# The first MLP product of a decoder layer by one level of Strassen's algorithm, with its output and the residual kept in DRAM

## The chip, the cores and the metric

One core of a Trainium2 chip runs the whole program. The metric is device time in microseconds, the median of three runs. The profile of one more execution shows the core's engines: TensorE (PE, with its weight loads as PEld), VectorE (DVE), ScalarE (ACT), GpSimd (POOL) and SyncE (SP), which issues most DMAs.

## The reference

The reference is one layer of a hybrid decoder on 1024 prompt tokens and 64 sample tokens (8 sequences of 8), 1088 columns in all. Only the end of the layer matters here:

```
x = x + gt * (merged @ lp["w_out"])
sh, sc, gt = ada_mod(c, lp["w_ada_mlp"], lp["b_ada_mlp"])
h = rms_norm(x, lp["norm_mlp"]) * (1 + sc) + sh
x = x + gt * (jnp.square(jax.nn.relu(h @ lp["w_ff1"])) @ lp["w_ff2"])
y = rms_norm(x, W["norm_final"])
```

`x` has 1024 features, `w_ff1` is 1024 by 4096 and `w_ff2` 4096 by 1024, all in fp32.

## The kernel before

**Layout.** Features lie on the 128 partitions, tokens along the free axis: `x`, `h` and the merged branch are 8 tiles of 128 x 1088, the hidden activations 32. Every product is done in three passes: an fp32 operand is split into a high part (an ACT copy to fp32r) and a low part (a DVE or POOL subtraction), and `mm3` multiplies high by high, high by low and low by high into one PSUM bank. A product's 1088 columns go in three chunks of 364, 362 and 362 (`CH`). One output block of the first MLP product takes 8 input blocks x 3 chunks x 3 passes = 72 matmuls; 32 blocks make 2304. The second product also has 2304.

**Weights.** `weights` loads 128 x 512 through the SP queue and splits it. In the second phase four such split sets exist, so a set is loaded and split four jobs' halves ahead, into the buffers of the set that has just been used up.

**Order.** TensorE's instructions are in the order in which the Python program emits them; a small clock (`Pace`) that counts estimated matmul time decides while building where the steps of the generators (`norm2`, `ada`) fall between the matmuls. The order on the other engines and in the DMA queues is made by the framework's scheduler. Each engine and queue works strictly in its own order: an instruction that waits holds up those behind it.

**Second phase (`phase2`).** The merge (`or_job`) writes the split merged branch; `out_job(m, 0)` forms output block m of the out-projection for the first 726 columns, `out_job(m, 1)` for the last 362, and the result is added to the residual tiles `xr`, which stay in SBUF. `norm2(0)` and `norm2(1)` sum the squares of each part, and when the statistics have gone through TensorE (`stats`, `rms`), scale, modulate and split it. While `norm2(0)` works, TensorE does the 192 matmuls of `out_job(m, 1)`; while `norm2(1)` works, it does the first two chunks of three hidden blocks. After that the two MLP products alternate: four hidden blocks (`ff1_job`, whose `consume` applies ReLU, squares and splits each chunk straight from PSUM), then the second product of the four hidden blocks before (`ff2_jobs`), added to `xr`. The hidden blocks never leave SBUF. The last group of the second product runs in `last`, with the final norm behind it. `ada` forms the modulation vectors; its third part (`g == 2`, the MLP's gate) starts when `norm2(1)` is done.

**SBUF.** `hx` (16 tiles of 128 x 1088) holds the eight `xr` tiles and hidden blocks, `ma`/`mb` the split operands of 726 and 362 columns, `t` has 4 work tiles, `hid` 4. **PSUM.** Tags `mm` (4 banks), `w` (2) and `wc` (2) live for the whole program.

## Time and profile before

| | us |
|---|---|
| median of 3 runs (1751.83 to 1753.74) | 1752.13 |
| span of the profiled execution | 1744.2 |
| median less that span | 7.9 |
| merge (bound by loads of `d_th`), some 780 to 850 us | 70 |
| out-projection and norms, some 850 to 965 us | 115 |
| both MLP products, 965 us to the end | 779 |

The share of busy time in a row tells how long instructions of an engine were under way. A matmul's record lasts longer than the distance to the next one (matmuls overlap), so the pace of TensorE is read from the starts: from first to last start of a group, divided by the matmuls between. Idle time of an engine other than TensorE costs nothing as long as TensorE does not wait for it.

### The profile page before, as it was taken

To read this page: it belongs to the slowest core of one execution; us is meant where nothing else is said; L and a number is where in the kernel's file an instruction comes from. 1 tells how busy PE (TensorE), PEld (TensorE's weight loads), DVE (VectorE), ACT (ScalarE), POOL (GpSimd) and SP (SyncE) were. 2 spreads that over 40 slices of the span, in tenths; PEclk is the share of its full clock that TensorE was granted. 3 is DMA by queue.
4 is the path that set the end of the run, shared out by engine and by line. 5 is a ranking of instruction groups with operands and counts; after the bars stand their busy time and mean duration, and the time that the engine had idled before them with its cause. 6 is when DMAs were issued, how large, how long until landed. Compare 5 with 4: busy or idle time off the path is not lost.

```text
span 1744.2 us, 32136 instructions
## 1 busy us (share of the span) xinstructions
PE 1686.4 (97%) x13462; PEld 1573.4 (90%) x13462; DVE 845.4 (48%) x1550; ACT 550.8 (32%) x1108; POOL 282.3 (16%) x379
## 2 busy tenths in 40 slices
PE   6999999999999999999899999999999999999997
PEld 3989879887888798799798999999999999999997
DVE  5677375746574654344337633324333333333355
ACT  5442343434343434122225521213121212212133
POOL 3310111000000000016215411111201111111121
PEclk9999999998999999999999999999999999999999
DMA  9333314232313332858742411111111111111112
GB/s 338 106 108 131 113 66 136 87 108 85 126 52 124 99 120 96 301 174 306 251 152 86 133 49 43 43 49 43 43 49 43 43 48 44 43 44 48 43 43 104
DMA packets 80785, 179.58 MB, mean 103 GB/s; under 512 B 11360, under 2 KB 25696, under 8 KB 80640
## 3 DMA queue, kind: packets, MB, share of 16 engines
q1 hardware_dynamic: 72960, 155.63, 26.5%
q10 hardware_dynamic: 6048, 16.23, 2.8%
q0 software_dynamic: 1632, 5.67, 1.0%
q8 instruction: 106, 1.74, 0.4%
q14 instruction: 39, 0.32, 0.1%
HBM read 138.64 MB, written 38.84 MB: 102 GB/s over the span
## 4 chain that ended last, share of the span: by engine, by line
PE 87%; DVE 6%; DMA 3%; ACT 2%; issue 1%; POOL 1%; SPq 0%; ACTq 0%; DVEq 0%; POOLq 0%
PE mm L170 58%; PE w L170 23%; PE wc L170 4%; DMA t<-d_th 2%; PE w L177 1%; POOL t L1344 1%; DMA x<-in_xT 1%; DVE t L1403 0%; DMA hid<-in_w_ada_mlp 0%; DVE ma L1405 0%; DVE mb L1348 0%; DVE wt L680 0%; DVE wlo L190 0%; DVE h L461 0%; DVE acc L1383 0%
## 5 line engine op out<-in xcount | busy, mean ns | idle before, releaser
L170 PE MATMUL mm<-hx,whi 128*128 128x362 f32 (+2 forms) x2608 | 679.6, 342 | 4.3 <-ACT px L564 1.6
L170 PEld LDWEIGHTS mm<-hx,whi 128*128 128x128 f32 x2608 | 455.8, 190 | 40.9 <-issue 17.8
L170 PE MATMUL mm<-hx,wlo 128*128 128x362 f32 (+3 forms) x1304 | 428.9, 329 | 0.0
L189 ACT ACTIVATE whi<-wraw 128x512 fp32r<-128x512 f32 x246 | 155.1, 630 | 535.6 <-PE w L170 356.0
L170 PE MATMUL mm<-ma,whi 128*128 128x364 f32 (+1 forms) x1280 | 318.7, 330 | 3.1 <-ACT ma L1347 2.6
L170 PEld LDWEIGHTS mm<-hx,wlo 128*128 128x128 f32 x1304 | 248.4, 190 | 0.1
L170 PEld LDWEIGHTS mm<-ma,whi 128*128 128x128 f32 x1280 | 226.7, 188 | 12.1 <-issue 8.4
L190 POOL TENSOR_TENSOR wlo<-wraw,whi 128x512 fp32r<-128x512 f32 x91 | 120.0, 1319 | 669.7 <-ACT whi L189 669.7
L170 PE MATMUL mm<-ma,wlo 128*128 128x364 f32 (+1 forms) x640 | 210.4, 329 | 0.2 <-DVE wlo L190 0.2
L190 DVE TENSOR_TENSOR wlo<-wraw,whi 128x512 fp32r<-128x512 f32 x155 | 109.1, 704 | 207.9 <-ACT whi L189 207.6
L1552 DVE SCALAR_TENSOR_TENSOR hx<-mm,aq,hx 128x364 f32<-128x364 f32 (+3 forms) x136 | 75.0, 587 | 206.5 <-PE mm L170 206.4
L170 PE MATMUL w<-mb,whi 128*128 128x362 f32 x576 | 143.8, 331 | 0.0
L170 PEld LDWEIGHTS mm<-ma,wlo 128*128 128x128 f32 x640 | 120.6, 189 | 0.5 <-DVE wlo L190 0.5
L1427 DVE TENSOR_TENSOR ft<-ft 128x362 f32<-128x362 f32 (+1 forms) x96 | 53.1, 576 | 130.3 <-ACT ft L1426 129.8
L170 PEld LDWEIGHTS w<-mb,whi 128*128 128x128 f32 x576 | 102.6, 191 | 2.5 <-issue 1.7
L170 PE MATMUL w<-hx,whi 128*128 128x362 f32 x416 | 102.8, 328 | 0.1
L170 PE MATMUL w<-mb,wlo 128*128 128x362 f32 x288 | 95.5, 332 | 2.7 <-DVE wlo L190 2.7
L170 PE MATMUL mm<-hid,whi 128*128 128x364 f32 (+4 forms) x304 | 74.9, 328 | 0.0
L170 PEld LDWEIGHTS w<-hx,whi 128*128 128x128 f32 x416 | 73.2, 189 | 1.3 <-POOL hx L466 0.8
L1426 ACT ACTIVATE ft<-mm 128x364 f32<-128x364 f32 x64 | 29.5, 475 | 125.5 <-PE mm L170 125.4
L170 PE MATMUL w<-hx,wlo 128*128 128x362 f32 x208 | 67.4, 324 | 0.0
L1557 POOL TENSOR_TENSOR hx<-hx,rs 128x64 f32<-128x64 f32 x72 | 39.3, 546 | 143.2 <-DVE rs L1555 143.1
(330 smaller groups left out, 2173.1 us busy)
## 6 DMA issues: line engine op xcount, KB each, us to landing
wraw<-in_w_ff SPq DMA_DIRECT2D x134, 256.0 KB, 2.6
wraw<-in_w_in SPq DMA_DIRECT2D x68, 256.0 KB, 3.0
hid<-in_w_ada_mlp SPq DMA_DIRECT2D x24, 512.0 KB, 4.5
d_th<-px SPq DMA_DIRECT2D x22, 544.0 KB, 3.0
wt<-d_x SPq DMA_DIRECT2D x20, 544.0 KB, 4.3
t<-d_th ACTq DMA_DIRECT2D x16, 544.0 KB, 6.4
aw<-in_w_ada_mix SPq DMA_DIRECT2D x16, 512.0 KB, 9.2
wraw<-in_w_out SPq DMA_DIRECT2D x32, 256.0 KB, 2.9
```

Of the source, the lines that this page charges most:

```text
L170: return self.nc.tensor.matmul(out, lhsT, rhs, **kw)
L177: self.nc.tensor.transpose(out, in_, ident)
L189: nc.scalar.activation(hi, raw, AF.Copy)
L190: (nc.gpsimd if n < 2 or n % 2 and n >= self.solo else nc.vector).tensor_tensor(lo, raw, hi.bitcast(F32), op=ALU.subtract)
L1344: nc.gpsimd.tensor_tensor(t, t, S["u"], op=ALU.add)
L1426: nc.scalar.activation(t[:, :n], ps[:, :n], AF.Relu)
L1427: nc.vector.tensor_tensor(t[:, :n], t[:, :n], t[:, :n], op=ALU.mult)
L1552: nc.vector.scalar_tensor_tensor(x[:, c0:c0 + m], ps[:, :m], gt[:, 0:1], x[:, c0:c0 + m], op0=ALU.mult, op1=ALU.add)
L1557: nc.gpsimd.tensor_tensor(x[:, NPR:NT], x[:, NPR:NT], t, op=ALU.add)
```

## The change

The 32 hidden blocks are taken in 16 pairs, and the 1088 columns in two halves of 544 (`HF`), each done as two matmuls of 272 (`HQ`). Call A11, A12 the two halves (512 inputs each) of the first block's weights in a pair, A21, A22 those of the second; B11, B21 the two feature halves of `h` for the first 544 columns, B12, B22 for the last 544. The seven half-size products (numbered as in the code), in Winograd's form, with every operand formed in fp32 first and then split, are:

- 0: A11 B11; 1: A12 B21;
- 5: (A21+A22-A11)(B22-B12+B11); 6: (A11-A21)(B22-B12); 4: (A21+A22)(B12-B11);
- 2: (A12-(A21+A22-A11)) B22; 3: A22 (B22-B12+B11-B21).

Products 0 and 1 accumulate in the same PSUM pair of banks, with product 0 copied out in between (`u`). The hidden block 2j is P0+P1 and P0+P5+P4+P2, the block 2j+1 is P0+P5+P6-P3 and P0+P5+P6+P4; VectorE forms these sums as it reads PSUM, ScalarE applies ReLU and then squares in place. A pair takes 7 x 4 x 2 x 3 = 168 matmuls of 272 columns.

The out-projection is cut at 544, too (two chunks of 272 in each half). `norm2(0)` forms and splits B11 and B21 in place of `xr`'s first half, `norm2(1)` forms B12, B22, the four combinations and splits these (20 splits). Products 0 and 1 of the first four pairs (`NE`, 8 products) are emitted before the others, as they need `norm2(0)` alone.

Since `xr` is overwritten, `norm2` first writes it to DRAM (`d_xr`, in halves), and it is loaded again at the end of the first product. The hidden blocks are written to DRAM (`d_hid`) in fp32, loaded again one group of four ahead and split then (`hidden`). The second product runs after the whole first one (`order2`), in the same chunks of 364, 362 and 362 as before. PSUM: `wc` has a pool of its own, the other six banks are given out anew for each stage, in the first product as three pairs of banks (`pr`). The third part of `ada` waits for the fourth pair instead of `norm2(1)`. `weights` is parted in two; its second half, `halves`, splits any raw tile.

The diff, cut (`MR` gives a pair of halves of tag `mr`, 16 tiles; `T` one of the 4 tiles `t`; `half` one of these, 544 wide; `HX` one of the 16 `hx` tiles):

```diff
     def ps(self, tag):
-        return self.pp.tile([P, 512], F32, tag=tag, bufs=self.pb[tag], name=self.nm(tag))
-
-    def stream(self, jobs, order=None):
+        return (self.pc if tag == "wc" else self.pp).tile([P, 512], F32, tag=tag, bufs=PB[tag], name=self.nm(tag))
+
+    def ps2(self):
+        return self.pp.tile([P, 2, 512], F32, tag="pr", bufs=3, name=self.nm("pr"))
+
+    def psum(self, ctx):
+        self.pp = ctx.enter_context(self.tc.tile_pool(name=self.nm("pp"), bufs=2, space=PSUM, reuse_waits="tile"))
...
+    def pair(self, pool, tag, bufs, n=None, dt=F32R):
+
+        t = pool.tile([P, 2, HF], dt, tag=tag, bufs=bufs, name=self.nm(tag))
+        return t[:, 0, :n], t[:, 1, :n]
...
+            self.d_xr, self.d_hid = scratch("d_xr", 8), scratch("d_hid", 32)
+            self.pc = ctx.enter_context(tc.tile_pool(name="pc", bufs=2, space=PSUM))
...
+        C = {}
+
+        def parts(c, k, src, pool=False):
+            hi, lo = C[c, k] = self.pair(self.hx, "hx", 16) if c < 2 else self.pair(p, "t", 4) if c == 3 else MR()
+            nc.scalar.activation(hi, src, AF.Copy)
+            (nc.gpsimd if pool else nc.vector).tensor_tensor(lo, src, hi.bitcast(F32), op=ALU.subtract)
...
         def norm2(i):
+            a, b = i * HF, (i + 1) * HF
...
                 yield lambda: ("out", m, i) in self.done
+                nc.sync.dma_start(self.d_xr[m][:, a:b], self.xr[m][:, a:b])
+                t = half() if m else acc
                 nc.scalar.activation(t, self.xr[m][:, a:b], AF.Square)
...
+            if i == 0:
+                self.mod_scale(g2, self.aq, "norm_mlp")
+            r = half()
+            yield from self.rms(po, 0, bl, r)
+            x = [t[:, a:b] for t in self.xr]
+            for k in range(4):
+                for kb in (k, k + 4):
+                    if i == 0:
+                        nc.vector.scalar_tensor_tensor(x[kb], x[kb], g2[:, kb, 0:1], r, op0=ALU.mult, op1=ALU.mult)
+                        nc.scalar.activation(x[kb], x[kb], AF.Identity, bias=self.aq[:, kb, 0:1])
+                        parts(kb // 4, k, x[kb], kb == 7)
+                        yield 1500
+                    else:
+                        nc.vector.tensor_tensor(x[kb], x[kb], r, op=ALU.mult)
+                        self.modulate(x[kb], x[kb], g2, self.aq, kb, a, HF, a)
+                if i:
+                    b11, b21 = self.xr[k][:, :HF], self.xr[k + 4][:, :HF]
+                    nc.vector.tensor_tensor(b11, x[k], b11, op=ALU.subtract)
+                    if k % 2 == 0:
+                        t2 = T().rearrange("p (s n) -> p s n", s=2)
+                    w = t2[:, k % 2]
+                    nc.vector.tensor_tensor(w, x[k + 4], b11, op=ALU.subtract)
+                    parts(5, k, w)
+                    nc.gpsimd.tensor_tensor(x[k], x[k + 4], x[k], op=ALU.subtract)
+                    nc.gpsimd.tensor_tensor(b21, w, b21, op=ALU.subtract)
+                    yield 2500
             if i:
-                r = acc
+                self.done.add(("C", 5))
+                for c, src in ((6, lambda k: x[k]), (4, lambda k: self.xr[k][:, :HF]), (2, lambda k: x[k + 4]), (3, lambda k: self.xr[k + 4][:, :HF])):
+                    for k in range(4):
+                        parts(c, k, src(k))
+                    self.done.add(("C", c))
+                    yield 1500
+            self.done.add(("h2", i))
...
+        def product(ps, c, w, first, last):
+            for k in range(4):
+                xh, xl = C[c, k]
+                for q in range(2):
+                    s = slice(q * HQ, (q + 1) * HQ)
+                    o, f, l = ps[:, q, :HQ], first and k == 0, last and k == 3
+                    self.mm(o, w[k][0], xh[:, s], start=f, stop=False, skip_group_check=True)
+                    self.mm(o, w[k][0], xl[:, s], start=False, stop=False, skip_group_check=True)
+                    self.mm(o, w[k][1], xh[:, s], start=False, stop=k == 3, skip_group_check=True)
+                    yield
+
+        def pair_steps(j, early):
+
+            D, S = {}, {}
+            src = lambda i, h: io["w_ff1"][2 * j + i][:, h * 512:(h + 1) * 512]
+
+            def raw(key, i, h):
+                self.nr += 1
+                q, tag, bufs = (self.wp, "wraw", 2) if self.nr % 3 == 0 else (p, "wr2", 4)
+                t = D[key] = q.tile([P, 512], F32, tag=tag, bufs=bufs, name=self.nm(tag))
+                if i is not None:
+                    nc.sync.dma_start(t, src(i, h))
+                return t
+
+            def prep(c):
+                def go():
+                    if c == 0:
+                        return self.halves(raw("a", 0, 0), False)
+                    if c == 5:
+                        if early == 2:
+                            raw("a", 0, 0)
+                        b, cc = raw("b", 1, 0), raw("c", 1, 1)
+                        nc.vector.tensor_tensor(cc, b, cc, op=ALU.add)
+                        d = raw("d", None, None)
+                        nc.vector.tensor_tensor(d, cc, D["a"], op=ALU.subtract)
+                        nc.gpsimd.tensor_tensor(b, D["a"], b, op=ALU.subtract)
+                        return self.halves(d, False)
+                    if c == 1:
+                        return self.halves(raw("e", 0, 1), False)
+                    if c == 6:
+                        return self.halves(D["b"], False)
+                    if c == 4:
+                        return self.halves(D["c"], False)
+                    if c == 2:
+                        e = raw("e", 0, 1) if early == 2 else D["e"]
+                        nc.gpsimd.tensor_tensor(e, e, D["d"], op=ALU.subtract)
+                        return self.halves(e, True)
+                    return self.halves(raw("f", 1, 1), True)
+                return go
+
+            def relu2(o):
+                nc.scalar.activation(o, o, AF.Relu)
+                nc.scalar.activation(o, o, AF.Square)
+
+            def run(c):
+                def go(w):
+                    if c in (0, 1):
+                        ps = S["x"] = S["x"] if c else self.ps2()
+                        yield from product(ps, c, w, c == 0, c == 1)
+                        v = ps[:, :, :HQ]
+                        if c == 0:
...
+                            nc.scalar.activation(v2(S["u"]), v, AF.Copy)
+                        else:
+                            nc.scalar.activation(v2(S["o"]), v, AF.Relu)
+                            nc.scalar.activation(S["o"], S["o"], AF.Square)
+                            if early:
+                                nc.sync.dma_start(self.d_hid[2 * j][:, :HF], S["o"])
+                        return
+                    ps = self.ps2()
+                    yield from product(ps, c, w, True, True)
+                    v = ps[:, :, :HQ]
+                    if c == 5:
...
+                        nc.vector.tensor_tensor(v2(S["u"]), v2(S["u"]), v, op=ALU.add)
+                    elif c == 6:
+                        nc.vector.tensor_tensor(v2(S["u1"]), v2(S["u"]), v, op=ALU.add)
+                    elif c == 4:
+                        o = S["o1"] = HX(F32)
+                        nc.vector.tensor_tensor(v2(S["u"]), v2(S["u"]), v, op=ALU.add)
+                        nc.vector.tensor_tensor(v2(o[:, HF:]), v2(S["u1"]), v, op=ALU.add)
+                        relu2(o[:, HF:])
+                    elif c == 2:
+                        o = S["o0"]
+                        nc.vector.tensor_tensor(v2(o[:, HF:]), v2(S["u"]), v, op=ALU.add)
+                        relu2(o[:, HF:])
+                        if early:
+                            nc.sync.dma_start(self.d_hid[2 * j][:, HF:], o[:, HF:])
+                        else:
+                            nc.sync.dma_start(self.d_hid[2 * j], o)
+                    else:
+                        o = S["o1"]
+                        nc.vector.tensor_tensor(v2(o[:, :HF]), v2(S["u1"]), v, op=ALU.subtract)
+                        relu2(o[:, :HF])
+                        nc.sync.dma_start(self.d_hid[2 * j + 1], o)
+                        self.done.add(("hid", j))
+                return go
+
+            return {c: (prep(c), run(c), c, j) for c in range(7)}
+
...
+        early, steps = [pair_steps(j, 1) for j in range(NE)], []
+        for j in range(0, NE, 2):
+            steps += [early[j][0], early[j + 1][0], early[j][1], early[j + 1][1]]
+        for j in range(16):
+            st = pair_steps(j, 2 if j < NE else 0)
+            steps += [st[c] for c in ((5, 6, 4, 2, 3) if j < NE else (0, 5, 1, 6, 4, 2, 3))]
+        todo = list(steps)
+        made = []
+
+        def more():
+            if todo:
+                made.append(todo.pop(0)[0]())
             else:
+                self.load2()
+
+        def ff1():
+            for _, run, c, j in steps:
+                while ("C", c) not in self.done and c > 1:
+                    yield "idle"
+                yield from run(made.pop(0))
+                more()
+                if j == 15 and c == 1:
+                    for m in range(8):
+                        self.xr[m] = HX(F32)
+                        nc.sync.dma_start(self.xr[m], self.d_xr[m])
+                if (j, c) in ((15, 5), (15, 6)):
+                    hidden(0, 2 * (c - 5))
 
...
+        def hidden(grp, part=None):
+            for j in range(4) if part is None else (part, part + 1):
+                raw, hi, lo = self.row(p, "hid", 4), self.row(p, "mr", 16, F32R), self.row(p, "mr", 16, F32R)
+                nc.sync.dma_start(raw, self.d_hid[4 * grp + j])
+                nc.scalar.activation(hi, raw, AF.Copy)
+                (nc.gpsimd if j == 3 else nc.vector).tensor_tensor(lo, raw, hi.bitcast(F32), op=ALU.subtract)
+                hid[4 * grp + j] = hi, lo
...
+        order2 = []
+        for grp in range(7):
+            for m, j in enumerate(ff2_jobs(grp)):
+                order2 += U(j)
+                if m == 0:
+                    order2.append((lambda g=grp + 1: iter([hidden(g)][:0]), 0))
+
+        def back():
+            with ExitStack() as c:
+                self.psum(c)
+                yield from self.stream(None, order, more)
+            with ExitStack() as c:
+                self.psum(c)
+                second, self.load2 = self.stream(None, order2, None, 0)
+                yield from ff1()
+            self.psum(self.ctx)
+            yield from second
+
+        self.pace.run(back(), [norm2(0), norm2(1), ada()])
...
+HF = NT // 2
+HQ = HF // 2
+QH = [[(0, HQ), (HQ, HQ)], [(HF, HQ), (HF + HQ, HQ)]]
...
+NE = 4
```

More of the change, by code (lines that the diff above doesn't have):

```diff
@@ L210, in load @@
                 W[id(j), h] = self.weights(j.halves[h])
+            elif more:
+                more()
+        if ahead == 0:
+            return self.products(flat, W, load), load
         for _ in range(4 if self.deep else 2):
@@ L1305, in phase2 @@
         HX = lambda dt=F32R: self.row(self.hx, "hx", 16, dt)
-        MG = lambda i: self.row(p, "m" + "ab"[i], 16, F32R, (CUT, NT - CUT)[i])
+        MR = lambda: self.pair(p, "mr", 16)
+        split = [slice(0, HF), slice(HF, NT)]
         TG = ("mm", "mm", "w")
@@ L1344, in after @@
                 nc.gpsimd.tensor_tensor(t, t, S["u"], op=ALU.add)
-                hi, lo = [(MG(0), MG(1)) for _ in range(2)]
-                for i, s in enumerate((slice(0, CUT), slice(CUT, NT))):
+                hi, lo = zip(*[MR() for _ in range(2)])
+                for i, s in enumerate(split):
                     nc.scalar.activation(hi[i], t[:, s], AF.Copy)
@@ L1565, in weights_rows @@
         for h in range(2):
-            hi, lo = (self.row(self.p2, "ma", 16, F32R, CUT)[:, :512] for _ in range(2))
+            hi, lo = self.pair(self.hx, "hx", 16, 512)
             raw = self.wp.tile([P, 512], F32, tag="wraw", bufs=WB[0], name=self.nm("wraw"))
@@ L1604 @@
 WARM = 1700
+PB = {"mm": 4, "w": 2, "wc": 2}
 FCH = [(640, 448), (256, 384), (0, 256)]
+NE = 4
 _OUTS = [("o_y", (8, P, NT)), ("o_ns", (P, 14, 9)), ("o_np", (P, 4, 9, 15)), ("o_wp", (4, P, 64)), ("o_ws", (4, P, 512))]
```

109 lines of the change are left out of this document (32 added, 77 removed).

## The prediction

> **What bounds the kernel now.** The page comes first: the busy shares, then the chain of waits.
>
> ```profile
> span 1744.2 us, 32136 instructions
> PE 1686.4 (97%) x13462; PEld 1573.4 (90%) x13462; DVE 845.4 (48%) x1550; ACT 550.8 (32%) x1108; POOL 282.3 (16%) x379
> ...
> PE mm L170 58%; PE w L170 23%; PE wc L170 4%; DMA t<-d_th 2%; PE w L177 1%; POOL t L1344 1%; DMA x<-in_xT 1%; DVE t L1403 0%; DMA hid<-in_w_ada_mlp 0%; DVE ma L1405 0%; DVE mb L1348 0%; DVE wt L680 0%; DVE wlo L190 0%; DVE h L461 0%; DVE acc L1383 0%
> ```
>
> The chain is matmuls on line 170 nearly throughout; the reader sees that the time falls when TensorE has less to do, as long as the others keep up. The view by windows gives the pace and the one soft spot; its columns are the window's length, each engine's busy time with its number of instructions, the granted clock, the DMA share and GB/s.
>
> ```profile
> core 0: us, PE busy (x) PEld busy (x) DVE busy (x) ACT busy (x) POOL busy (x), PEclk, DMA share, GB/s
> 941.84:951.43 9.59, 6.55 (x28) 5.95 (x28) 9.59 (x14) 5.30 (x9) 5.54 (x5) 0.82 0.21 66
> 966.11:982.36 16.25, 16.25 (x100) 16.25 (x99) 16.22 (x25) 13.71 (x30) 13.78 (x20) 1.00 0.18 58
> 1100.00:1200.00 100.00, 100.00 (x605) 100.00 (x604) 34.59 (x65) 21.26 (x41) 14.27 (x16) 1.00 0.14 45
> 1728.08:1732.31 4.23, 4.23 (x38) 4.23 (x37) 3.37 (x5) 2.18 (x5) 4.17 (x4) 1.00 0.24 88
> ```
>
> In the MLP stage (third row) the clock is whole, DVE a third busy, and a matmul starts every 100/605 = 0.1653 us, at 362.7 columns on average. The first row is the second half of the out-projection, where `norm2(0)` crowds DVE: 27 matmuls, worth 27 x 0.1653 = 4.5 us, took 9.59. So 5.1 us are lost there, 3.0 of them waiting and the rest at a granted clock below 1. Another 1.0 us goes in front of `norm2(1)`'s statistics. The list of TensorE's waits from the merge on has the longest of these:
>
> ```profile
> PE w L170 <- DVE wlo L190: 2.7, 1, 2.7
> ```
>
> **The first product's matmuls.** Removed are 2304 x 0.1653 = 380.8 us. Added are 16 x 168 = 2688 matmuls of 272 columns, a width that the kernel does not have. Near it lie the 256 columns of the last group; the timeline of TensorE has the first and the last of seven groups of six:
>
> ```profile
> 1728.08 0.86 PE L170 MATMUL mm<-hx,ma 128*128 128x256 f32 x6
> ...
> 1732.31 0.87 PE L170 MATMUL mm<-hx,ma 128*128 128x256 f32 x6
> ```
>
> Start to start, 4.23 us/36 = 0.1175 us, with the same three passes and a weight load for each matmul. So a shorter matmul is still paid by its columns, and the weight loads stay behind it. Between the two widths a column costs (0.1653 - 0.1175)/106.7 = 0.00045 us, which puts 272 at 0.1247 (in proportion to the wider ones 0.1240, to the narrower ones 0.1248). 2688 x 0.1247 = 335.1 us: **-45.7** (-45.2 to -47.5). The eighth that the algorithm saves comes through almost whole.
>
> The out-projection has 768 matmuls of 272 for 576 of 362.7: 95.8 - 95.2 = **+0.6**.
>
> **The first norm.** `norm2(0)` now has 384 matmuls of cover (47.9 us) instead of 192 (31.7), and 544 columns to treat, not 726. The 5.1 us lost there may go or stay; DVE still has eight scalings in a row ahead of a weight split that TensorE waits for, so I leave 2 of them. With the 1.0 us above: **-4.1** (-6.1 to -1.0).
>
> **The second norm: where a new stall comes.** The old cover was 144 matmuls and what followed needed eight splits. The new one is 8 products, and then each of products 5, 6, 4, 2, 3 of the first pair needs four fresh splits. The start of the chain is in the timeline: the last out-projection matmul, the statistics, the first scaling.
>
> ```profile
> 954.76 0.33 PE L170 MATMUL mm<-mb,wlo 128*128 128x362 f32 x1
> ...
> 956.89 0.83 PE L170 MATMUL wc<-kct,acc 128*128 128x3 f32 x6 [0.85 <-DVE acc L1383]
> ...
> 966.11 3.07 DVE L1407 TENSOR_TENSOR t<-hx,acc 128x362 f32<-128x362 f32 x4 [1.52 <-ACT acc L326]
> ```
>
> From 954.93 to 966.11 are 11.2 us; less the wait of 0.85, DVE starts 10.3 us after the out-projection. TensorE's cover is 8 x 24 x 0.1247 = 23.9 us, with fifteen small matmuls at 0.83/6 us 26.0; product 3 of the first pair would end at 26.0 + 5 x 3.0 = 41.0. In the changed program's order, DVE has 49 instructions from its first scaling to the weight split without which the second pair cannot go on: 40 of 544 elements (8 scalings, 8 combinations, 20 low parts, 4 evictions) and 9 of 512 (weights), 26,368 elements. POOL has 16 of 64 elements, 8 of 544 and 4 of 512 beside it. Prices, from the list of groups (last columns: total busy and mean ns of one):
>
> ```profile
> L190 DVE TENSOR_TENSOR wlo<-wraw,whi 128x512 fp32r<-128x512 f32 x155 | 109.1, 704 | 207.9 <-ACT whi L189 207.6
> L190 POOL TENSOR_TENSOR wlo<-wraw,whi 128x512 fp32r<-128x512 f32 x91 | 120.0, 1319 | 669.7 <-ACT whi L189 669.7
> L361 POOL TENSOR_TENSOR t<-t,g 128x64 f32<-128x64 f32 x8 | 4.6, 590 | 4.3 <-DVE t L1407 4.3
> L362 POOL TENSOR_TENSOR t<-t,aq 128x64 f32<-128x64 f32 x8 | 4.4, 558 | 0.2
> L189 ACT ACTIVATE whi<-wraw 128x512 fp32r<-128x512 f32 x246 | 155.1, 630 | 535.6 <-PE w L170 356.0
> L1381 ACT ACTIVATE t<-hx 128x726 f32<-128x726 f32 x8 | 6.5, 812 | 1.1 <-DVE hx L1552 0.5
> L1552 DVE SCALAR_TENSOR_TENSOR hx<-mm,aq,hx 128x362 f32<-128x362 f32 x56 | 32.8, 586 | 0.0
> ```
>
> In quiet, DVE takes 704/512 = 1.375 ns an element, 36.3 us in all. Beside a busy POOL it is slower; the nearest such place is the old second norm, 966.11 to 982.36 (second row of the windows), where DVE did this:
>
> ```profile
> L1407 DVE TENSOR_TENSOR t<-hx,acc 128x362 f32<-128x362 f32 x8 | 5.9, 782 | 1.5 <-ACT acc L326 1.5
> L1410 DVE TENSOR_TENSOR mb<-t,mb 128x362 fp32r<-128x362 f32 x6 | 3.6, 611 | 0.0
> L1427 DVE TENSOR_TENSOR ft<-ft 128x362 f32<-128x362 f32 x2 | 2.3, 1128 | 0.0
> L190 DVE TENSOR_TENSOR wlo<-wraw,whi 128x512 fp32r<-128x512 f32 x2 | 2.1, 1047 | 0.0
> L1427 DVE TENSOR_TENSOR ft<-ft 128x364 f32<-128x364 f32 x2 | 1.3, 632 | 0.0
> L1429 DVE TENSOR_TENSOR hx<-ft,hx 128x362 fp32r<-128x362 f32 x2 | 1.3, 626 | 0.0
> L1429 DVE TENSOR_TENSOR hx<-ft,hx 128x364 fp32r<-128x364 f32 x2 | 1.2, 584 | 0.0
> ```
>
> That is 24 instructions, 8,996 elements in 16.25 us: 1.806 ns each, 47.6 us for the 49. TensorE then stands for 10.3 + 47.6 - 41.0 = 16.9 us. In quiet it is 5.6; if DVE and POOL wholly exclude each other, POOL's 9.2 + 11.2 + 5.3 = 25.7 us come on top of the quiet time: 31.3. I take the crowded pace, as the work is of the same kind, and 2 us for the clock after it (as the first row lost 2.1): **+19** (6 to 34).
>
> **Hidden blocks and residual through DRAM.** Written and read again are 32 hidden blocks and 8 residual tiles, 80 x 0.557 = 44.6 MB over some 750 us, 59 GB/s beside the 45 in the third window, where the DMA share is 0.14. All are SP's; a write waits there for ReLU and square, and the next weight loads stand behind it, but these are four products (12 us) ahead of use. Reads are issued a group (47 us) ahead, except the first group's, which wait for the buffers of products 5 and 6 of the last pair. Their splits are ACT's and DVE's 1088 columns and one of POOL's:
>
> ```profile
> L1119 ACT ACTIVATE wt<-wt 128x1088 fp32r<-128x1088 f32 x3 | 3.3, 1113 | 8.4 <-DVE wt L1100 8.4
> L1120 DVE TENSOR_TENSOR wt<-wt,wt 128x1088 fp32r<-128x1088 f32 x3 | 3.9, 1292 | 3.9 <-ACT wt L1119 3.9
> L1344 POOL TENSOR_TENSOR t<-t,t 128x1088 f32<-128x1088 f32 x8 | 21.8, 2725 | 15.2 <-DVE t L1340 6.1 <-DMA t<-d_th 4.3 <-DVE wlo L190 3.1
> ```
>
> The longest chain, 2 x 1.1 + 2.7 = 4.9 us after product 6, lies under products 4, 2 and 3 (9 us). For the change of PSUM pools I add **+1.5** (0 to 5).
>
> **Inside the first product.** A pair lasts 168 x 0.1247 = 20.9 us on TensorE. DVE has 6 evictions of 544 (586 ns at 362, so some 0.8) and 7 of 512: 9.7 us. ACT has 7 splits of 0.63 and 9 passes of 544, 0.66 by rows at 512 and 726: 10.4. POOL has 4 x 1.32 = 5.3. All are hidden at half load, so nothing is added; were that cover gone, the price is in the third rival.
>
> **Sum.** 1744.2 - 45.7 + 0.6 - 4.1 + 19 + 1.5 = 1715.5, and the 7.9 us by which the runs' median exceeds the span, unchanged: **1723 us**, 1.7% faster.
>
> **Rivals.** *Quiet transition.* DVE keeps its quiet pace: 5.6 us of stall and 1 of clock, nothing lost in the first norm or at the pools: 1744.2 - 45.7 + 0.6 - 6.1 + 6.6 + 7.9 = 1707 or 1708. For it: most of POOL's 64-wide work is over before the combinations. Against: eight POOL subtractions of 544 then begin.
>
> *Full exclusion.* Of DVE and POOL one waits whole instructions for the other. The timeline has such a pair:
>
> ```profile
> 977.05 1.59 POOL L190 TENSOR_TENSOR wlo<-wraw,whi 128x512 fp32r<-128x512 f32 x1
> 977.40 1.63 DVE L1427 TENSOR_TENSOR ft<-ft 128x362 f32<-128x362 f32 x1
> ```
>
> DVE ends just after POOL and takes 1.63 us for what takes 0.6 elsewhere. With 31.3 us of stall, 3 of clock, the first norm's 5.1 kept and 3 at the pools: 1744.2 - 45.7 + 0.6 - 1.0 + 34.3 + 3 + 7.9 = 1743. Against: in the window above both were busy nearly all of the 16 us. The Trainium skill has this as a rule (SBUF — State Buffer, "SBUF: two separate sides"): the two engines lock a shared port pair for the whole instruction, DVE with two SBUF inputs among them; the pair of rows agrees, and by the rule this rival would be the forecast.
>
> *Slower: the PSUM handoffs inside a pair.* Product 1 accumulates onto product 0 only after ACT's copy, and product 4 takes the banks that ACT frees after product 1; each has one product, 3.0 us, to hide in. ACT needs a split (0.63) and the copy (0.66), 1.3 us, so 1.7 are spare, if ACT is not held up behind a ReLU whose sum DVE forms late. At 1.5 us late for each of the 32 handoffs the time is 1723 + 48 = 1771; from 0.9 us each the change is a loss. Against: the half loads above.
>
> **How the numbers follow.** Forecast 0.48, quiet 0.22, exclusion 0.15, handoffs 0.12, and 0.03 for a sum that lands on the old time. The first three lie from 1703 to 1746 with their bounds (1707 less the matmuls' end; 1743 plus the pools' end): the range, with 0.15 left out. Within 0.2% (3.5 us) is what a measurement can't tell from no change: 0.03. Faster: 0.85; slower: 0.12.
>
> **What would show it.** Right, if 2688 matmuls of 272 start some 0.125 us apart in the steady pairs, TensorE's waits are gathered within 60 us of the out-projection's end, on DVE's low parts, and the clock dips there alone. The size of the stall tells the first three cases apart. Wrong, if matmuls of 272 start 0.14 us apart or more, or TensorE waits for ACT in each pair.

## The result, and the profile after

The kernel after took 1712.24 us (median of 4 runs, 1711.73 to 1712.70); the kernel before, beside it, 1752.93 (1751.83 to 1757.21). The ratio is 0.9769, 95% interval 0.9751 to 0.9788: 40.7 us faster. The forecast was 1723 us, 11 more than measured, inside its range.

The page of the kernel after, first the busy shares of the engines and then the chain of waits:

```profile
span 1710.4 us, 33795 instructions
PE 1641.9 (96%) x14043; PEld 1527.6 (89%) x14043; DVE 918.5 (54%) x1586; ACT 628.1 (37%) x1150; POOL 369.8 (22%) x421
...
PE mm L170 48%; PE pr L170 18%; PE w L170 17%; PE wc L170 4%; PE w L177 1%; DMA x<-in_xT 1%; DMA hid<-in_w_ada_mlp 0%; DVE mr L1395 0%; DVE wlo L194 0%; DVE bk L712 0%; POOL hx L380 0%; DVE wt L699 0%; POOL hx L381 0%; DVE h L480 0%; DVE hx
```

TensorE is still the chain. It has 581 matmuls more (384 for the first product, 192 for the out-projection, 5 others) and is busy for 44.5 us less, because they are shorter. The other three engines work more than before and stay far from full. By windows (columns as in the prediction):

```profile
core 0: us, PE busy (x) PEld busy (x) DVE busy (x) ACT busy (x) POOL busy (x), PEclk, DMA share, GB/s
900.00:955.00 55.00, 55.00 (x445) 54.01 (x445) 32.24 (x57) 25.36 (x44) 15.55 (x15) 1.00 0.41 142
980.00:990.00 10.00, 5.20 (x38) 4.54 (x36) 10.00 (x7) 5.10 (x9) 10.00 (x7) 1.00 0.12 45
990.00:1000.00 10.00, 7.75 (x36) 6.92 (x37) 10.00 (x11) 8.89 (x17) 4.75 (x3) 0.66 0.17 57
1000.00:1010.00 10.00, 7.05 (x54) 6.80 (x55) 10.00 (x13) 1.89 (x4) 6.80 (x4) 1.00 0.21 68
1100.00:1200.00 100.00, 100.00 (x806) 100.00 (x805) 49.80 (x62) 49.23 (x78) 27.87 (x20) 1.00 0.33 119
...
1200.00:1250.00 50.00, 50.00 (x404) 50.00 (x403) 25.32 (x33) 24.48 (x39) 11.59 (x9) 1.00 0.31 109
...
1400.00:1500.00 100.00, 100.00 (x608) 100.00 (x607) 40.99 (x83) 19.47 (x25) 25.15 (x27) 1.00 0.28 90
```

The fifth and sixth rows are the steady first product: TensorE without a gap at the whole clock. The counts in such a row take in the matmuls under way at both of its edges (100/806 is 0.1241 us, 50/404 is 0.1238), so the pace is read from starts. These are the first matmuls of two pairs, eight pairs or 8 x 168 = 1344 matmuls apart:

```profile
1104.60 0.41 PE L170 MATMUL pr<-hx,whi 128*128 128x272 f32 x2
...
1271.85 0.41 PE L170 MATMUL pr<-hx,whi 128*128 128x272 f32 x2
```

That is 167.25/1344 = 0.1244 us a matmul and 20.9 us a pair, as predicted. VectorE and ScalarE are half loaded, as worked out. Rows two to four are the place that the prediction called the new stall: TensorE busy for 20.0 of 30 us, VectorE for all of them. The list of TensorE's waits, over the whole run, has these from there on (us in total, times, the longest):

```profile
PE pr L170 <- DVE mr L1395: 6.6, 3, 4.3
PE pr L170 <- POOL wlo L194: 2.9, 1, 2.9
```

How long that transition lasts is read from the last matmul of the out-projection and the first of the second pair's product 5 (the first `pr<-mr` after those that read `t`):

```profile
955.28 0.29 PE L170 MATMUL mm<-mr,wlo 128*128 128x272 f32 x1
...
1012.24 0.41 PE L170 MATMUL pr<-mr,whi 128*128 128x272 f32 x2
```

From 955.57 to 1012.24 are 56.7 us for work that was costed at 41.0: 15.7 us are lost.

### The profile page after: what moved, and what is told of

It is laid out like the page before. It is cut to its first block, busy times and chain, and to the rows that moved or that the text cites. A ratio compares the mean times of both kernels' runs of the same rounds, so it can differ in the third digit from the quotient of the medians.

```text
span 1710.4 us, 33795 instructions
## 1 busy us (share of the span) xinstructions
PE 1641.9 (96%) x14043; PEld 1527.6 (89%) x14043; DVE 918.5 (54%) x1586; ACT 628.1 (37%) x1150; POOL 369.8 (22%) x421
## 4 chain that ended last, share of the span: by engine, by line
PE 88%; DVE 5%; ACT 2%; issue 2%; DMA 1%; POOL 1%; SPq 0%; DVEq 0%; ACTq 0%; POOLq 0%
PE mm L170 48%; PE pr L170 18%; PE w L170 17%; PE wc L170 4%; PE w L177 1%; DMA x<-in_xT 1%; DMA hid<-in_w_ada_mlp 0%; DVE mr L1395 0%; DVE wlo L194 0%; DVE bk L712 0%; POOL hx L380 0%; DVE wt L699 0%; POOL hx L381 0%; DVE h L480 0%; DVE hx L1691 0%
## 5 line engine op out<-in xcount | busy, mean ns | idle before, releaser
L170 PE MATMUL mm<-hx,whi 128*128 128x362 f32 (+1 forms) x1920 | 507.1, 346 | 6.4 <-ACT px L565 2.9
L170 PEld LDWEIGHTS mm<-hx,whi 128*128 128x128 f32 x1920 | 333.4, 190 | 43.6 <-issue 18.9
L170 PE MATMUL mm<-mr,whi 128*128 128x364 f32 (+4 forms) x1504 | 345.9, 318 | 3.1 <-ACT mr L1369 2.0
L170 PE MATMUL mm<-hx,wlo 128*128 128x362 f32 (+1 forms) x960 | 316.0, 329 | 0.0
L170 PEld LDWEIGHTS mm<-mr,whi 128*128 128x128 f32 x1504 | 255.2, 189 | 11.7 <-issue 7.4
L170 PE MATMUL mm<-mr,wlo 128*128 128x364 f32 (+4 forms) x752 | 235.5, 313 | 0.0
L170 PE MATMUL pr<-mr,whi 128*128 128x272 f32 x1024 | 196.4, 290 | 7.1 <-DVE mr L1395 6.6
L170 PEld LDWEIGHTS pr<-mr,whi 128*128 128x128 f32 x1024 | 162.6, 190 | 10.2 <-DVE mr L1395 8.0
L170 PE MATMUL pr<-mr,wlo 128*128 128x272 f32 x512 | 148.5, 290 | 2.9 <-POOL wlo L194 2.9
L170 PEld LDWEIGHTS mm<-mr,wlo 128*128 128x128 f32 x752 | 143.3, 191 | 0.2
```

What stands on the lines that cost most here:

```text
L170: return self.nc.tensor.matmul(out, lhsT, rhs, **kw)
```

## The experiments

Two numbers are taken from each trace: the *transition*, as just read, and the *tail*, from the same end of the out-projection to the end of the span. Each comes from one execution, but they repeat far better than the whole time: the kernel after gave 56.7 and 754.8 us twice, the kernel before a tail of 789.1 and 790.5. The table gives both; "ratio" is against the kernel before on the same chip.

| run | median us (lowest to highest) | ratio, 95% interval | transition | tail |
|---|---|---|---|---|
| the profiled run before / after | | | | 789.1 / 754.8 |
| e1_before | 1747.19 (1742.51 to 1754.51) | 0.9976 to 1.001 | | 790.5 |
| e5_after | 1715.26 (1708.39 to 1719.17) | 0.9796 to 0.9851 | 56.7 | 754.8 |
| e2_two_pairs | 1725.32 (1717.52 to 1729.83) | 0.9846 to 0.9885 | 55.3 | 765.6 |
| e3_combos_dve | 1711.82 (1709.50 to 1715.40) | 0.9763 to 0.9801 | 57.4 | 755.4 |
| e12_splits_alone | 1715.32 (1709.98 to 1719.23) | 0.9773 to 0.9828 | 59.0 | 757.0 |
| e8_no_gpsimd | 1705.78 (1703.91 to 1710.26) | 0.9732 to 0.9785 | 52.5 | 750.9 |
| e4_two_accumulators | 1713.81 (1711.64 to 1717.40) | 0.9774 to 0.9812 | 59.9 | 760.3 |
| e7_plain_eight | 1745.66 (1742.73 to 1746.83) | 0.9967 to 0.9994 | | 788.1 |
| e10_written_twice | 1712.92 (1712.07 to 1715.51) | 0.9764 to 0.9815 | 56.7 | 755.0 |
| e6_eight_pairs | 1711.35 (1706.24 to 1713.21) | 0.9754 to 0.9809 | 78.5 | 755.0 |
| e9_eight_pairs_no_gpsimd | 1701.81 (1700.94 to 1705.80) | 0.9700 to 0.9752 | 73.1 | 747.8 |
| e11_copies_moved | 1698.62 (1696.90 to 1704.41) | 0.9690 to 0.9739 | 69.4 | 744.2 |

### What lies outside the span, and how far runs agree

The kernel before, with no edit:

> The kernel before, unchanged, for the time and the span of the same executions. Theory A: its profiled execution was a short one, and in every execution the time is 1.8 us more than the span, as in the kernel after (1712.16 for a span of 1710.4): spans of 1750 to 1752 for times of 1752 to 1754. Theory B: the kernel before loses time outside its span that the kernel after doesn't: spans near 1744.2 and times some 7.9 us above them.

Theory A holds, though the spans spread wider than it said. The profiled execution took 1754.51 us with a span of 1752.7, the shortest 1742.51 with 1740.7: 1.8 us lie outside in each of ten runs. The 7.9 us that the prediction added were no cost outside the span; the execution profiled first was a short one of a kernel whose time moves by 12 us from run to run.

The kernel after, with no edit, beside the runs on its chip:

> The kernel after, unchanged, beside the following kernels. It should have 1710 to 1714 us, a time 1.8 us above its span, and 56 to 57 us from the end of the out-projection to the start of the second pair's product 5, where the matmuls alone would take 41.0.

Transition and tail are those of the first profile to 0.1 us. The times scatter more than expected (1708.39 to 1719.17), and the traces show where: the last matmul of the out-projection starts at 952.06 us in this profile, at 955.28 in the first one and at 960.17 in e12_splits_alone, whose edit lies behind that point. The two kernels are 33.0 us apart here (1748.30 and 1715.26), where the first measurement had 40.7. What the change does must be read from the tail: 789.1 and 790.5 us before, 754.8 and 754.8 after, 34.3 to 35.7 us less.

### Is the transition a matter of cover?

```
-NE = 4
+NE = 2
```

> Two pairs instead of four go ahead with their products 0 and 1, so TensorE has four products (4 x 24 x 0.124 = 11.9 us) less to do while the second norm is worked out. Theory: the stall of 15.8 us is what VectorE's chain exceeds this cover by; the stall grows by 11.9 us less the four weight splits that the chain no longer has ahead (4 x 0.7 = 2.8 us at most): 1721 to 1724 us. Rival: the stall is one of a weight's transfer or of GpSimd, not of the cover: 1712 to 1715.

The median is 1725.32 us, 1.3 above the theory's range, but the tail grows by 765.6 - 754.8 = 10.8 us, between the 9.1 and the 11.9 expected. The transition takes 55.3 us for work of 29.1, so the loss grew from 15.7 to 26.2. What TensorE has to do while VectorE works counts almost in full.

### What slows VectorE there?

The timeline of VectorE and GpSimd in the kernel after (start, duration, engine, line, operation, count):

```profile
978.59 0.81 DVE L1435 TENSOR_TENSOR t<-hx,hx 128x544 f32<-128x544 f32 x1
...
981.09 1.87 DVE L1435 TENSOR_TENSOR t<-hx,hx 128x544 f32<-128x544 f32 x1
982.89 3.58 DVE L1395 TENSOR_TENSOR mr<-t,mr 128x544 fp32r<-128x544 f32 x2
...
999.67 1.35 DVE L1395 TENSOR_TENSOR mr<-hx,mr 128x544 fp32r<-128x544 f32 x2
```

```profile
978.16 0.66 POOL L381 TENSOR_TENSOR hx<-hx,aq 128x64 f32<-128x64 f32 x1
978.78 3.60 POOL L1437 TENSOR_TENSOR hx<-hx,hx 128x544 f32<-128x544 f32 x2
982.34 1.81 POOL L1438 TENSOR_TENSOR hx<-t,hx 128x544 f32<-128x544 f32 x1
...
991.15 3.61 POOL L1438 TENSOR_TENSOR hx<-t,hx 128x544 f32<-128x544 f32 x2
```

The same subtraction of VectorE takes 0.81 us beside GpSimd's 64-column work, 1.87 beside its 544-column work, and 0.7 after that has ended. From 979 to 995 us some nine instructions of VectorE took 1.8 us. The eight subtractions were moved:

```
-                    nc.gpsimd.tensor_tensor(x[k], x[k + 4], x[k], op=ALU.subtract)
-                    nc.gpsimd.tensor_tensor(b21, w, b21, op=ALU.subtract)
+                    nc.vector.tensor_tensor(x[k], x[k + 4], x[k], op=ALU.subtract)
+                    nc.vector.tensor_tensor(b21, w, b21, op=ALU.subtract)
```

> The eight GpSimd subtractions of 544 columns in the second norm go to VectorE. Theory (the two engines exclude each other for whole instructions): some nine VectorE instructions in 979 to 995 us took 1.8 us each where they take 0.7 alone, 10 us lost; moved, the eight cost 8 x 0.66 = 5.3 us on VectorE and one such pair with a weight's subtraction stays (1.1 us): 3 to 4 us faster than the kernel after, 1708 to 1709.5. Rival (VectorE is slow there for another reason, its load counts alone): 5.3 us are added, 1717 to 1718.

The reason was right and the gain did not come: a transition of 57.4 us, and a median of 1711.82, between the two cases. VectorE's and then GpSimd's and SyncE's timelines of this run show both halves of that:

```profile
990.40 0.71 DVE L1395 TENSOR_TENSOR t<-hx,t 128x544 fp32r<-128x544 f32 x1
991.04 0.71 DVE L1395 TENSOR_TENSOR mr<-t,mr 128x544 fp32r<-128x544 f32 x1
...
994.18 1.98 DVE L1395 TENSOR_TENSOR mr<-hx,mr 128x544 fp32r<-128x544 f32 x3
1000.69 0.69 DVE L1483 TENSOR_TENSOR wr<-wr,wr 128x512 f32<-128x512 f32 x1 [4.53 <-DMA wr<-in_w_ff]
```

```profile
988.54 8.77 POOL L194 TENSOR_TENSOR wlo<-wr,whi 128x512 fp32r<-128x512 f32 x1 [4.92 <-ACT whi L193]
```

```profile
997.33 0.33 SPq L1472 DMA_DIRECT2D wr<-in_w_ff  x1
```

VectorE's instructions are down to 0.71 us, so the slowness was GpSimd's doing. But the one low part that GpSimd still has in that stretch takes 8.77 us: it ends at 997.31, 1.15 us after VectorE's row of work has ended. SyncE's next weight load is issued at 997.33, at once behind it, and VectorE then stands 4.53 us for a load, with the splits that TensorE needs queued behind. So that split, of the first pair's product 2, and its neighbour of product 3 were moved as well:

```
-                        return self.halves(e, True)
-                    return self.halves(raw("f", 1, 1), True)
+                        return self.halves(e, early != 2 or j)
+                    return self.halves(raw("f", 1, 1), early != 2 or j)
```

> The eight GpSimd subtractions of 544 columns go to VectorE, as in the run with these alone, and so do the two weight splits of the first pair's products 2 and 3. In that run one of those splits took 8.8 us on GpSimd while VectorE worked without a break; the weight loads behind its buffer came that much later, and VectorE then waited 4.5 us for one of them. Theory (that wait is what ate the gain): it goes, for 2 x 0.68 us more on VectorE, and the stretch from the out-projection's end to the second pair's product 5 falls from 57.1 to 53 to 55 us. Rival (VectorE's own work sets the end): 57 to 59 us.

Transition 52.5 us, tail 750.9, 3.9 less than in the kernel after: even a little more than expected. To see whether the subtractions matter at all, the splits alone were moved:

> Of the two moves from GpSimd to VectorE only the second: the two weight splits of the first pair's products 2 and 3; the eight subtractions of 544 columns stay on GpSimd. Theory (the two moves pay separately: the subtractions by what they lock VectorE, the splits by a wait of 2.9 us for GpSimd's low part): the 2.9 us go and 1.3 come on VectorE, the stretch from the out-projection's end to the second pair's product 5 falls from 56.4 to 54 to 56 us, against 52.0 with both. Rival (the subtractions never mattered, and the splits alone make the gain): 52 to 53 us.

Both guesses missed: the transition is 59.0 us, 2.3 longer than with neither move. The list of TensorE's waits of this run says what became of the 2.9 us:

```profile
PE pr L170 <- DVE mr L1395: 6.7, 3, 4.3
PE pr L170 <- DVE wlo L194: 3.7, 1, 3.7
```

The 4.3 us behind the locked splits are still there, and the low part now comes late from VectorE, where it starts at 1011.30 behind a weight sum (1010.70) in the same queue, instead of from GpSimd. So the two moves do not add up: alone they cost 0.7 and 2.3 us of transition, together they gain 4.2.

### Are the PSUM handoffs hidden?

```
-tag="pr", bufs=3
+tag="pr", bufs=2
```

> Two PSUM accumulators of two banks instead of three: every product now takes the banks of the product but one before it, with one product (3.0 us) to hide the eviction in. Theory (VectorE and ScalarE half loaded, an eviction done 0.7 to 1.4 us after its product): the handoffs stay hidden, 1712 to 1717. Rival (the third rival of the prediction: evictions come late by about a product's length): from 0.5 us at each of some 100 handoffs up, 1760 and more.

The median is 1713.81 us, inside the theory's range. From 1030 to 1300 us TensorE waits for nothing at all in this run. The tail is 5.5 us longer: 3.2 of them are in the transition, 0.7 are a wait just behind it and 1.0 more waiting at the end of the first product; the rest is not traced. The two longest waits, both in the transition, are these:

```profile
PE pr L170 <- DVE hid L1534: 6.6, 1, 6.6
PE pr L170 <- ACT hid L1519: 5.2, 1, 5.2
```

In the steady pairs a handoff thus fits into one product of 3.0 us even without the third accumulator. In the transition, where the evictions stand behind the norm's work, it doesn't.

### Are the trips through DRAM hidden?

```
                            nc.sync.dma_start(self.d_hid[2 * j], o)
+                            nc.sync.dma_start(self.d_hid2[2 * j], o)
```

and likewise behind the other three writes of hidden blocks.

> Every hidden block is written to DRAM a second time, to a scratch that nothing reads: 17.8 MB and 36 more transfers from SyncE's queue in the first product. Theory (the trips through DRAM are hidden): as the kernel after, within the scatter of its runs, 1708 to 1717 us, and no wait of TensorE for a weight in the steady pairs. Rival (SyncE's queue, where the weight loads stand behind the writes, has no room left): TensorE waits for weights in each pair, 1720 and more.

Tail 755.0 us against 754.8, and no wait of TensorE between 1010 us and the end of the first product. From 1100 to 1200 us the DMA share rises from 0.33 to 0.48 and TensorE has the same 806 matmuls. The trips are hidden, with room to spare.

### How much is the algorithm's, how much the stage's?

All of the product is computed, in the plain way. The core of the edit:

```
-            if i:
-                ...
-                for c, src in ((6, ...), (4, ...), (2, ...), (3, ...)):
+                        parts(2 + kb // 4, k, x[kb])
...
+                return lambda: self.halves(raw(c, c % 4 // 2, c % 2), c in (3, 7))
...
+                    i, b, part = c // 4, c % 4 // 2, c % 2
+                    ps = S["x"] = S["x"] if part else self.ps2()
+                    yield from product(ps, 2 * i + part, w, part == 0, part == 1)
...
-steps += [st[c] for c in ((5, 6, 4, 2, 3) if j < NE else (0, 5, 1, 6, 4, 2, 3))]
+steps += [st[c] for c in ((4, 5, 6, 7) if j < NE else range(8))]
```

with NE = 2, so that eight products go ahead as before.

> The stage of its own, the halves of 544 columns, the PSUM accumulators and the blocks through DRAM stay, but each pair of output blocks is made with the eight plain half-size products instead of the seven (3072 matmuls of 272 instead of 2688), without combinations of inputs, weights or results. Theory (the gain is the eighth of the products, less what the combinations cost in front of the first pair; the new stage itself costs nothing): 384 x 0.1238 = 47.5 us more and the loss of 15.8 us gone, 1742 to 1747, about the time before. Rival (part of the gain is the stage's, such as the wait-free order): under 1738; or the stage itself has a price that the algorithm hides: over 1752.

1745.66 us, and a tail of 788.1 against 789.1 and 790.5 before: the stage by itself, with the shorter matmuls and the blocks through DRAM, changes it by 1.0 to 2.4 us. The seven products for eight then bring 788.1 - 754.8 = 33.3 us. The matmuls saved are worth 384 x 0.1244 = 47.8 us. Of the 15.7 lost in the transition, 0.8 is a wait for VectorE to empty the out-projection's last bank, which this run has too, so 14.9 go off; and this run waits 0.6 us longer at the end of the first product. That makes 33.5, so the gain is accounted for.

### Can the loss be had back?

Eight pairs go ahead instead of four; what product 0 leaves makes a trip to DRAM:

```
-NE = 4
+NE = 8
...
+            self.d_u = scratch("d_u", 8)
...
+                            if early:
+                                nc.sync.dma_start(self.d_u[j][:, :HF], S["u"])
...
+                            Z[j] = self.pair(p, "hid", 4, dt=F32)
+                            nc.sync.dma_start(Z[j][0], self.d_u[j][:, :HF])
```

> Eight pairs instead of four go ahead with their products 0 and 1; as there are only four buffers for what product 0 leaves, it goes to DRAM too and comes back before product 5. TensorE has eight products (8 x 24 x 0.124 = 23.8 us) more to do while the second norm is worked out. Theory (the loss of 15.8 us is VectorE's chain against this cover): the chain grows by at most eight weight splits, 5.6 us, the cover by 23.8, so the loss goes: 1696 to 1700. Rival (the loss comes back at the next place, as the clock, a weight's transfer or a late read from DRAM): 1706 to 1712.

The rival came: 1711.35 us, tail 755.0, no gain; 13.6 us are still lost (78.5 less 64.9), and a wait of 1.5 us follows behind the transition. The waits for `mr` are gone, and others are in their place. ScalarE's timeline, and below it TensorE's two long waits:

```profile
981.04 0.66 ACT L1395 ACTIVATE t<-hx 128x544 fp32r<-128x544 f32 x1 [4.82 <-POOL hx L1439]
...
985.72 0.60 ACT L1526 ACTIVATE hid<-pr 128x544 f32<-128x544 f32 x1
986.38 5.04 ACT L1395 ACTIVATE mr<-hx 128x544 fp32r<-128x544 f32 x9
```

```profile
986.38 0.82 PE L170 MATMUL pr<-hx,whi 128*128 128x272 f32 x2 [3.39 <-ACT hid L1526]
...
995.16 0.82 PE L170 MATMUL pr<-hx,whi 128*128 128x272 f32 x2 [4.07 <-ACT hid L1522]
```

ScalarE stands 4.82 us for a GpSimd subtraction and then makes the norm's copies in one row; the early products' results, which only ScalarE takes out of PSUM, are queued behind both. With the edits of e8_no_gpsimd added:

> Eight pairs ahead and nothing of the second norm's 544-column work on GpSimd, both edits together. In the run with eight pairs ScalarE stood 4.8 us for a GpSimd subtraction, and then made its copies for the second norm in one row, while TensorE waited 3.4 and 4.1 us for PSUM that the early products' results, behind them on ScalarE, held. Theory: the first of these goes with the GpSimd work, the second stays with 14 copies of 0.55 us in a row (7.7 us, against two products of 3.0 before the accumulators are full: 2 to 4 us of waiting): from the out-projection's end to the first product 5 but one 67 to 71 us where the matmuls take 64.9, and 1698 to 1703 us. Rival (the loss is VectorE's or a weight's transfer after all): 75 us and more, 1706 to 1712.

1701.81 us, tail 747.8; the time is in the theory's range, the transition of 73.1 half-way between its 71 and the rival's 75. One wait is left, of 5.4 us for ScalarE, with the clock at 0.66 behind it. The copies for products 4 and 2 were then made on VectorE:

```
-            nc.scalar.activation(hi, src, AF.Copy)
+            if c in (4, 2):
+                nc.vector.tensor_copy(hi, src)
+            else:
+                nc.scalar.activation(hi, src, AF.Copy)
```

> As the run with eight pairs and no GpSimd work, and of ScalarE's twenty copies of 544 columns the eight for products 4 and 2 go to VectorE. Theory (TensorE's 5.4 us of waiting there, and the lower clock after it, come from ScalarE's row of 14 copies, behind which the early products' results stand): the row falls to some six copies (3.3 us), the wait to under 2 us, the stretch from the out-projection's end to the first product 5 but one from 72.7 to 65 to 69 us, the time to 1694 to 1699 us; VectorE's chain, some 57 us of 65 before, has room for eight copies of 0.6. Rival (VectorE becomes the bound): 72 us and more, 1701 and more.

1698.62 us, ratio 0.9715 (0.9690 to 0.9739), tail 744.2, the fastest of all; the transition, 69.4, is just outside what was expected. Windows of e9_eight_pairs_no_gpsimd (first fence) and of this run, both from 33.9 to 43.9 us behind the end of the out-projection:

```profile
990.00:1000.00 10.00, 5.85 (x30) 5.85 (x31) 10.00 (x17) 6.27 (x13) 0.00 (x0) 0.66 0.27 92
```

```profile
984.78:994.78 10.00, 8.86 (x71) 8.64 (x71) 10.00 (x21) 5.01 (x9) 0.00 (x0) 1.00 0.50 167
```

TensorE has 71 matmuls there instead of 30: less waiting, and a whole clock. What is left, 69.4 less 64.9, are short waits, the largest for low parts of weights on VectorE.

## Why the prediction was right, point by point

**The matmuls' price**, the largest term, was right in kind and small by 2.6 us. 272 columns were priced at 0.1247 us and cost 0.1244, which is 0.7 us over 2688. The rest lies in the old matmuls: the prediction's 100/605 counts those under way at the edges of its window. The kernel before takes 288 matmuls for four hidden blocks and then 288 of the second product; the first matmul of one such group, of the next and of the third are

```profile
1071.27 0.50 PE L170 MATMUL mm<-ma,whi 128*128 128x364 f32 x2
...
1119.12 0.49 PE L170 MATMUL mm<-hid,whi 128*128 128x364 f32 x2
...
1166.90 0.50 PE L170 MATMUL mm<-ma,whi 128*128 128x364 f32 x2
```

So a matmul of the first product took 47.85/288 = 0.1661 us, not 0.1653, and 2304 x 0.1661 - 2688 x 0.1244 = 48.3 us, 0.8 beyond the far bound of 47.5. The second product also went a little quicker: its groups of 288 start 47.57 us apart in the kernel after (1361.87 to 1409.44) and 47.6 to 47.8 before, about 1.2 us over eight groups, a term that the sum did not have.

**The second norm's stall** was there, at its place and nearly of its size: 15.7 us against 16.9 and 2 for the clock. VectorE started 11.2 us after the out-projection, as in the kernel before; the wait of 0.85 us that the prediction took off (10.3) did not come off. Then VectorE worked through 49 instructions, as counted, in 45.6 us instead of 47.6, and TensorE could begin the second pair's product 5 at 56.7 (57.9). The last wait of the transition is not on VectorE, as forecast, but the 2.9 us for a low part of GpSimd's. It decides next to nothing, because the 49th instruction, the low part of product 5's weights, ends at 1012.38 and TensorE reads it from 1012.49 on:

```profile
1011.70 0.68 DVE L194 TENSOR_TENSOR wlo<-wraw,whi 128x512 fp32r<-128x512 f32 x1
```

```profile
1012.49 0.34 PE L170 MATMUL pr<-mr,wlo 128*128 128x272 f32 x1
```

That the size came out so near was in part luck: two errors offset each other. The "crowded" 1.806 ns an element is no pace that holds throughout: eleven instructions took 1.8 us each, locked with GpSimd (nine from 979 to 995 us, two from 1005 to 1008.6), 19.4 us from start to start, and the other 38 took 0.69 on average, 26.2 us. In quiet, 544 columns start 0.64 us apart (990.40 and 991.04 in e3_combos_dve), where 1.375 ns an element makes 0.75; and the lock, spread over all 49 by the crowded pace, falls on eleven of them alone. And the 2 us for the clock should not have been added: VectorE sets when the next pair can start, so a TensorE that is slow on the way (0.66 from 990 to 1000 us) loses nothing more.

**Full exclusion**, the third case, was right about the mechanism and wrong about its extent. The Trainium skill's rule (SBUF — State Buffer, "SBUF: two separate sides"), that the two engines lock their shared port for a whole instruction, agrees with 1.87 us beside GpSimd's 1.81 and 0.71 alone. But of GpSimd's 25.7 us that were all added, its 64-column work hardly shows (VectorE 0.81 instead of 0.71), and only the 544-column row and a part of its weight work met VectorE instruction for instruction.

**The first norm.** From 900 to 955 us TensorE is busy without a gap at a whole clock, so the second half of the out-projection lost nothing: the term came to its favourable end, not to the -4.1 taken. In the two profiled spans this cannot be seen, for the out-projection's end moves by more than that from run to run in stages ahead of the change. Nor do the medians settle it, 40.7 us apart in one set and 33.0 in the other, where the tails are 34.3 to 35.7 apart.

**DRAM, and the inside of a pair**, at nothing: shown by e10_written_twice and e4_two_accumulators. **The pools' change** cost 0.3 us of waiting for VectorE's last sum, not 1.5; the 0.8 us of waiting for the out-projection's last bank, at the other change of pools, are in the 15.7. The handoff rival was wrong for the pairs, though handoffs are what bounds the transition once VectorE's chain is covered (e6_eight_pairs).

**Against the clock on the wall.** The tail fell by 34.3 us in the two profiles where the sum's terms after the out-projection come to -45.7 + 19 + 1.5 - 1.0 = -26.2. Of the 8.1 between, 2.6 are the matmuls, 1.2 the second product, 3.3 the stall with its clock and 1.2 the pools, 8.3 in all, 0.2 too many. Ahead of the tail the sum had 2.5 us less (0.6 - 3.1), and the profile after has 0.5 more, by the scatter of that stretch. So the span of 1710.4 is 5.1 below the sum's 1715.5. The other 6.1 of the miss of 11 are in the last term, "the 7.9 us by which the runs' median exceeds the span, unchanged": 1.8 us lie outside the span in both kernels, and 6.1 were the chance of a short profiled execution. With 1.8 the forecast would have been 1717.

This last term cancels in the difference between the kernels, and there the forecast was short as well: 28.7 us, against tails that are 34.3 to 35.7 apart. One figure of the range does not follow from its own sum: 1707.5 less the 1.8 of the matmuls' far bound is 1706, not 1703. The measured time lies within either.

## What to carry to other kernels

An algorithm that saves matmuls gives the saving almost whole where the other engines have room, and pays at the seam where its extra inputs are first made: cost that seam as one engine's in-order work against the matmuls that can cover it. When more cover is found, ask at once what else is queued on the in-order engines in that stretch, for the next limit here was PSUM results behind a row of copies on ScalarE. Compare kernels by a stretch of the trace that begins where the change begins, once a repeated run has shown how much the stages ahead of it move.

## What had not been expected of the hardware

- GpSimd not only slows VectorE: in e3_combos_dve, where VectorE had instructions back to back, one 512-column subtraction on GpSimd took 8.77 us (1.3 us on average before). In the kernel after the two took turns at 1.8 us each; the runs do not show why they alternated there and GpSimd was held off here.
- With a weight load for every matmul, a column cost the same at three widths: 0.1175/256 = 0.000459 us, 0.1244/272 = 0.000457 and, in the kernel before, (1166.90 - 1071.27)/576 = 0.1660 us for 362.7 columns, 0.000458.
- The granted clock was 0.52 from 992 to 998 us in the kernel after, behind its wait of 4.3 us, and stayed whole behind the one of 2.9 us, where TensorE was busy for 7.05 of 10 us. It also fell without a long wait: in e3_combos_dve, where TensorE worked 2.5 of the 5 us from 985 to 990 and waited 1.7 us at most up to 995, it was 0.64 from 990 to 995 and 0.67 in the next 5 us. The Trainium skill (TensorE: Matmul & The Clock Gate, "Part 1: The HAM clock gate (the "warmup" mystery)") has the clock follow how busy TensorE has lately been; these rows agree with that better than with a rule on the length of one wait.

Windows of the kernel after, and then of e3_combos_dve, for the last point:

```profile
992.00:998.00 6.00, 5.88 (x24) 5.24 (x25) 6.00 (x7) 6.00 (x12) 2.75 (x2) 0.52 0.01 1
```

```profile
985.00:990.00 5.00, 2.48 (x18) 2.04 (x16) 5.00 (x9) 4.82 (x10) 1.46 (x1) 1.00 0.18 55
990.00:995.00 5.00, 2.70 (x12) 2.15 (x11) 5.00 (x9) 5.00 (x11) 5.00 (x1) 0.64 0.14 55
995.00:1000.00 5.00, 4.34 (x23) 4.12 (x22) 1.16 (x2) 3.24 (x6) 2.30 (x1) 0.67 0.29 99
```

Twenty-four matmuls fill the 5.88 busy us of the first row, about twice what they take at a whole clock.
